# One rotation of eight tags for the operand tiles of the down projection

## The chip, the cores and the metric

The kernel runs on one core of a Trainium2 chip. Five engines work side by side, each through its own list of instructions in order: TensorE (PE) multiplies, ScalarE (ACT), VectorE (DVE) and GpSimd (POOL) work element by element, and SyncE's queue (SP) starts the transfers. Weight loads into TensorE are shown as PEld. The metric is the device time of one execution in microseconds. Three executions of the kernel before took 1674.23, 1678.88 and 1683.34 us; the median is 1678.88 us. One more execution was recorded by the profiler, and all rows below are from it.

## The reference

One encoder block over 1024 tokens of width 1024 in float32: two attentions, gated and merged, then a squared-ReLU MLP, then a gated embedding term and a last norm. The part that matters here is the MLP's second product:

```python
h2 = rmsnorm(x, g_mlp[i])
u = jax.nn.relu(jnp.einsum("bsd,df->bsf", h2, w_up[i]))      # w_up   1024 x 4096
x = x + jnp.einsum("bsf,fd->bsd", u * u, w_down[i])           # w_down 4096 x 1024
```

## The kernel before

Every float32 matrix product is done as three passes of a shorter format. An operand is split into a high part (a cast on ACT, line 1113) and a low part (the operand minus its high part, line 1114), and `mm3` (line 123) multiplies high by high, high by low and low by high into one PSUM sum.

The up projection writes the squared activations, and sums and differences of their blocks ("operand sums"), to a scratch tensor `u_d` in DRAM. The sums are made in five rotating SBUF tiles named `us`, in the pool `fp`; line 1062 sends them out.

The down projection walks over four chunks `c` of 1024 hidden columns. In each chunk Winograd's form of Strassen's scheme makes 7 block products in place of 8, in the order 1, 2, 5, 6, 3, 7, 4. A block product sums over four steps `k`; a step needs one left operand (`da`, from the tiles `ua` loaded from `u_d`) and one right operand (`db`, from `w_down` in the tiles `wd`, or from a sum or difference of its blocks that POOL makes in place, line 1200). Each operand, high and low part together, is one tile of the pool `dp`. A step is 12 matmuls of 512 columns, a block product is 48, all four chunks are 28 block products and 224 operand tiles. When a product is done, its PSUM sums are added to an accumulator `acc` on DVE (line 1144), or in chunk 0 for products 1, 5, 6 and 7 copied to it on ACT (line 1142). In the last chunk the accumulators are also added to one another on DVE and POOL (line 1093), and then the norm of the next stage begins (line 1101).

Operand tile number `n` (counted in program order, from 0) takes the tag `d0` to `d9` that line 1112 names. Every tag has one buffer, so a new tile of a tag waits until TensorE has finished with the old one. The pool `dp` is opened when `fp` is closed, and its tiles lie where `fp`'s tiles lay; the tiles that come to lie on `us` tiles can be written only when the transfers out of these have ended. A scheduler puts every engine's instructions into an order ahead of time, with its own estimate of when a tile is free; on the chip each engine then keeps to that order.

Where the text below says "pair k of product i", it means the two operand tiles of step k, `da` and `db`, with their two casts on ACT and two subtractions on DVE. In the first product of chunk 0 the first two pairs' subtractions are on POOL.

Of the kernel before, what the change touches and what calls it, by code (L numbers as in the profile page):

```python
# [10 lines left out]
F32R = mybir.dt.float32r  # L11
# [8 lines left out]
P = 128  # L20
# [33 lines left out]
def hybrid_block_kernel(ctx: ExitStack, tc, x, p, g_mix, w_in, g_qa, w_qb, g_kva, w_kvb, g_qn, g_kn,  # L54
# [34 lines left out]
    def raw_tile(name, shape):  # L89
        return wpool.tile(shape, F32, tag="raw", name=f"raw_{name}")  # L90
# [422 lines left out]
    with tc.tile_pool(name="ap", bufs=2, reuse_waits="tile") as ap:  # L513
# [273 lines left out]
        for i in range(NK + 2):  # L787
# [3 lines left out]
            d = i - 2  # L791
# [35 lines left out]
    with tc.tile_pool(name="op", bufs=2, reuse_waits="tile") as op:  # L827
# [115 lines left out]
        for n, f in enumerate((0, 2, 1)):  # L943
            t = raw_tile(f"early{f}", [P, NK, P])
# [162 lines left out]
    with tc.tile_pool(name="dp", bufs=1, reuse_waits="tile") as dp:  # L1107
        def operand(name, raw, eng):
            n = nd[0]
            nd[0] += 1  # L1110

            t = dp.tile([P, 2, 512], F32R, tag=f"d{n % 8 if n < 24 else (n - 16) % 10}", name=f"d{name}")
            act.copy(t[:, 0], raw)  # L1113
            eng.tensor_tensor(t[:, 1], raw, t[:, 0].bitcast(F32), ALU.subtract)  # L1114
            return t

        def product(i, c, av, bv):
# [34 lines left out]
            for k in range(4):  # L1152
                eng = pool if c == 0 and i == 1 and k < 2 else dve
                ab.append((operand(f"a{k}_{i}_{c}", av[k // 2][:, k % 2], eng), operand(f"b{k}_{i}_{c}", bv[:, k], eng)))
                if whole:
                    continue
                for s in range(4):
                    if k == 0:
                        room(s)
                    part(s, k, k + 1)  # L1160
                    if k == 3:
                        put(s)
# [205 lines left out]
```

## Time and profile before

| | |
|---|---|
| median of three runs | 1678.88 us (1674.23 to 1683.34) |
| the profiled execution | 1672.75 us, its span 1671.0 us |
| PE busy | 1559.7 us, 93% of the span |
| DVE busy | 1215.2 us, 73% |
| ACT busy | 815.5 us, 49% |
| POOL busy | 730.1 us, 44% |
| mean granted TensorE clock | 0.974 of 2.4 GHz |

The span runs from the first to the last instruction, and the other 1.75 us of the execution lie around it. Times in the rows count from the start of the span. The down projection runs from about 1197 us to about 1534 us. A granted clock of 1.00 is 2.4 GHz, one of 0.50 is 1.2 GHz, and a value between them is a mean over a stretch that has both.

### The profile page before, as it was taken

Reading aid. Unit: us, or ns where it says so; the run is one execution under the profiler, and the core shown is the slowest. Engines: PE = TensorE matmul, PEld = TensorE weight load, DVE = VectorE, ACT = ScalarE, POOL = GpSimd, SP = SyncE. Lnnn points to the kernel's source line nnn. Section 1 sums busy time; section 2 is a strip of 40 time slices with the busy share of each in tenths; the row PEclk is TensorE's granted clock in tenths of the full one; section 3 lists DMA queues with packets and bytes.
Section 4 is the critical chain, followed back from the end, with each engine's and each line's share of the span. In section 5 each row is a group of like instructions: output and inputs, shape, how many; then the busy total and the mean of one; then the engine's idle time right before and its main releaser. Section 6 shows DMA issues by size and latency. Waiting matters only on the chain.

```text
span 1671.0 us, 24113 instructions
## 1 busy us (share of the span) xinstructions
PE 1559.7 (93%) x8490; PEld 1320.2 (79%) x8490; DVE 1215.2 (73%) x1967; ACT 815.5 (49%) x1583; POOL 730.1 (44%) x463
## 2 busy tenths in 40 slices
PE   7999989998989888899996999999969999998898
PEld 6998877776767566688995888888758888877898
DVE  7278227776888888655467999999666878898753
ACT  6344337776988787533354222222245444435443
POOL 4254004645777777422154433333521322254653
PEclk9999999999999998999997999999979999999999
DMA  6023558999999999945544444444946353311242
GB/s 228 26 51 109 142 160 169 213 186 201 207 180 195 201 191 199 244 150 189 174 131 125 158 157 150 158 141 140 374 148 228 101 189 110 139 64 64 89 130 73
DMA packets 437865, 262.56 MB, mean 157 GB/s; under 512 B 284520, under 2 KB 383472, under 8 KB 437360
## 3 DMA queue, kind: packets, MB, share of 16 engines
q1 hardware_dynamic: 436464, 258.92, 59.2%
q10 hardware_dynamic: 1280, 2.10, 0.6%
q8 instruction: 67, 1.10, 0.3%
q14 instruction: 54, 0.44, 0.1%
HBM read 142.41 MB, written 49.35 MB: 115 GB/s over the span
## 4 chain that ended last, share of the span: by engine, by line
PE 48%; DMA 12%; DVE 10%; ACT 5%; issue 4%; POOL 4%; SPq 1%; POOLq 0%; ACTq 0%; DVEq 0%
PE u L126 17%; PE d L126 15%; DMA PT<-hl 7%; PE y L126 4%; PE wo L126 4%; PE pg L126 3%; POOL hl L602 2%; PE av L772 2%; PE gt L126 1%; ACT p L594 1%; ACT hl L600 1%; DMA wd<-in_w_down_dram 1%; DVE db L1114 1%; DVE p L591 1%; DMA bc<-rs_d 1%
## 5 line engine op out<-in xcount | busy, mean ns | idle before, releaser
L602 POOL TENSOR_TENSOR hl<-p,hl 128x1024 f16<-128x1024 f32 x128 | 279.8, 2193 | 194.8 <-PE gt L126 80.5
L126 PE MATMUL d<-db,da 128*128 128x512 f32 x1344 | 312.6, 395 | 23.3 <-ACT db L1113 16.6
L126 PEld LDWEIGHTS d<-db,da 128*128 128x128 f32 x1344 | 255.8, 191 | 79.4 <-ACT db L1113 17.0
L126 PE MATMUL u<-H_t,wop 128*128 128x512 f32 x768 | 183.6, 395 | 5.8 <-ACT H_t L900 4.6
L126 PEld LDWEIGHTS u<-H_t,wop 128*128 128x128 f32 x768 | 146.1, 191 | 38.2 <-ACT H_t L900 5.0
L591 DVE TENSOR_SCALAR_CACHE_REDUCE p<-s 128x1024 f32<-128x1024 f32 x128 | 155.6, 1218 | 16.1 <-PE s L126 5.6
L1113 ACT CAST da<-ua 128x512 fp32r<-128x512 f32 x112 | 69.6, 623 | 174.6 <-PE d L126 142.9
L594 ACT ACTIVATE p<-p,mx 128x1024 f32<-128x1024 f32 x128 | 147.2, 1150 | 9.5 <-DVE Va L458 1.5
L126 PE MATMUL u<-H_b,wop 128*128 128x512 f32 x576 | 138.2, 393 | 7.2 <-ACT wop L815 7.2
L126 PEld LDWEIGHTS u<-H_b,wop 128*128 128x128 f32 x576 | 109.4, 190 | 30.4 <-ACT wop L815 7.6
L1114 DVE TENSOR_TENSOR da<-ua,da 128x512 fp32r<-128x512 f32 x110 | 90.0, 819 | 58.2 <-ACT da L1113 58.2
L1200 POOL TENSOR_TENSOR wd<-wd,wd 128x1024 f32<-128x1024 f32 x16 | 39.8, 2492 | 195.3 <-DVE db L1114 187.4
L601 DVE TENSOR_SCALAR_CACHE_REDUCE hl<-p 128x512 f16<-128x512 f32 x128 | 87.2, 681 | 49.2 <-DMA PT<-hl 34.5
L1114 DVE TENSOR_TENSOR db<-wd,db 128x512 fp32r<-128x512 f32 x110 | 113.5, 1032 | 0.0
L126 PE MATMUL s<-KT,QT 96*128 96x512 f32 x384 | 103.5, 410 | 7.1 <-DVE p L591 6.8
L1057 POOL TENSOR_TENSOR us<-uq 128x512 f32<-128x512 f32 x15 | 19.6, 1308 | 192.9 <-DVE uq L1053 192.9
L126 PE MATMUL gt<-hH,lo_g 128*128 128x512 f32 x256 | 102.4, 400 | 1.5 <-DVE lo_g L105 1.5
L126 PE MATMUL gt<-hH,hi_g 128*128 128x512 f32 x256 | 101.9, 398 | 0.8 <-ACT hi_g L103 0.8
L126 PE MATMUL gt<-hL,hi_g 128*128 128x512 f32 x256 | 101.2, 395 | 0.0
L105 DVE TENSOR_TENSOR lo_g<-raw_g,hi_g 128x1024 fp32r<-128x1024 f32 x32 | 46.1, 1441 | 66.9 <-ACT hi_g L103 66.8
L600 ACT CAST hl<-p 128x512 f16<-128x512 f32 x128 | 78.7, 616 | 27.4 <-DMA PT<-hl 25.5
L126 PEld LDWEIGHTS s<-KT,QT 96*128 96x128 f32 x384 | 69.6, 193 | 25.2 <-DVE p L591 10.0
(341 smaller groups left out, 3930.7 us busy)
## 6 DMA issues: line engine op xcount, KB each, us to landing
ua<-u_d SPq DMA_DIRECT2D x56, 512.0 KB, 3.8
raw_g<-in_w_in_dram SPq DMA_DIRECT2D x32, 512.0 KB, 4.2
raw_up<-in_w_up_dram SPq DMA_DIRECT2D x32, 512.0 KB, 4.8
u_d<-us SPq DMA_DIRECT2D x64, 256.0 KB, 2.1
wd<-in_w_down_dram SPq DMA_DIRECT2D x16, 1024.0 KB, 9.7
u_d<-uq SPq DMA_DIRECT2D x48, 256.0 KB, 2.0
gates_d<-gst SPq DMA_DIRECT2D x32, 256.0 KB, 2.7
gg<-gates_d SPq DMA_DIRECT2D x16, 512.0 KB, 3.1
```

The source lines that it names most:

```text
L105: eng.tensor_tensor(lo, raw, hi.bitcast(F32), ALU.subtract)
L126: return [pe.matmul(ps, a, b, start=start and i == 0, stop=stop and i == len(m) - 1) for i, (a, b) in list(enumerate(m))[first:last]]
L591: dve.tensor_scalar(e, ps, 1.0, 3e38, op0=ALU.mult, op1=ALU.min, accum_out=mx)
L594: act.activation(e, e, AF.Exp, bias=mx, scale=-1.0, accum_out=sums[:, hd, qt:qt + 1])
L600: act.copy(hl[:, 0, :CUT], e[:, :CUT])
L601: dve.tensor_scalar(hl[:, 0, CUT:], e[:, CUT:], 1.0, 0.0, op0=ALU.mult, op1=ALU.max, accum_out=top)
L602: pool.tensor_tensor(hl[:, 1], e, hl[:, 0], ALU.subtract)
L772: pe.matmul(av[:, :256], values(hd, kt), PT[(2 * g + half) % 3][:, n, kt], start=(kt + n == 0), stop=(kt + n == NS))
L1057: eng.tensor_tensor(v[1], q[:, 2], q[:, 3], ALU.add)
L1113: act.copy(t[:, 0], raw)
L1114: eng.tensor_tensor(t[:, 1], raw, t[:, 0].bitcast(F32), ALU.subtract)
L1200: pool.tensor_tensor(o[:, ks], a[:, ks], b[:, ks], ALU.subtract)
```

## The change

All operand tiles now take the eight tags `d0` to `d7` in turn. Before, that held for the first 24 tiles (products 1, 2 and 5 of chunk 0); the tiles after them took ten tags in turn, beginning with `d8` and `d9`. The tiles `d8` and `d9` no longer exist.

```diff
         def operand(name, raw, eng):
             n = nd[0]
             nd[0] += 1
-
-            t = dp.tile([P, 2, 512], F32R, tag=f"d{n % 8 if n < 24 else (n - 16) % 10}", name=f"d{name}")
+            t = dp.tile([P, 2, 512], F32R, tag=f"d{n % 8}", name=f"d{name}")
             act.copy(t[:, 0], raw)
             eng.tensor_tensor(t[:, 1], raw, t[:, 0].bitcast(F32), ALU.subtract)
             return t
```

The scheduler orders the instructions anew. In the names below the digit behind `da` or `db` is the step k, the next one the product, the next one the chunk: `da0_6_0` is the left operand of step 0 of product 6 in chunk 0. Lines have moved up by one.

ACT, the casts from the end of product 1 of chunk 0 on, before:

```order
L1113 CAST db2_1_0_11597<-wd0_0_11295 128x512
L1113 CAST da3_1_0_11612<-ua0_11294 128x512 [waits DVE_49]
L1113 CAST db3_1_0_11615<-wd0_0_11295 128x512 [waits Pool_49]
L1113 CAST da0_6_0_11796<-ua2_0_0_11549 128x512 [waits DMAHW3_49,DMAHW4_49,DMAHW2_49,DMAHW5_49,DMAHW0_49,DMAHW6_49,DVE_49,Pool_49]
L1113 CAST da0_2_0_11634<-ua0_11294 128x512 [waits PE_49,Pool_49]
```

And the same place with the change:

```order
L1112 CAST db2_1_0_11597<-wd0_0_11295 128x512
L1112 CAST da3_1_0_11612<-ua0_11294 128x512 [waits DVE_49]
L1112 CAST db3_1_0_11615<-wd0_0_11295 128x512 [waits Pool_49]
L1112 CAST da0_2_0_11634<-ua0_11294 128x512 [waits DMAHW6_49,PE_49,Pool_49]
L1112 CAST db0_2_0_11637<-wd0_0_11295 128x512 [waits DMAHW1_49,Pool_49]
```

The cast for tile 24 (product 6, the first tile with tag `d8`) stood ahead of all casts of product 2 and waited for six transfer semaphores; with the change it stands behind all casts of product 5.

DVE in the last chunk, from the adds of product 2 to the first pair of product 3, before (`acc0<-acc0,d2` is the add of product 2's sum):

```order
L1144 TENSOR_TENSOR acc0_11537<-acc0_11537,d2_3_2_13419 128x1024
L1114 TENSOR_TENSOR da0_6_3_13576<-ua2_3_0_13320,da0_6_3_13576 128x512
...
L1114 TENSOR_TENSOR da2_6_3_13614<-ua2_3_1_13322,da2_6_3_13614 128x512
L1114 TENSOR_TENSOR db2_6_3_13617<-wd3_0_12738,db2_6_3_13617 128x512
L1144 TENSOR_TENSOR acc3_11541<-acc3_11541,d5_3_0_13496 128x512
L1114 TENSOR_TENSOR da3_6_3_13632<-ua2_3_1_13322,da3_6_3_13632 128x512
L1114 TENSOR_TENSOR db3_6_3_13635<-wd3_0_12738,db3_6_3_13635 128x512
L1144 TENSOR_TENSOR acc3_11541<-acc3_11541,d5_3_1_13500 128x512
...
L1114 TENSOR_TENSOR db0_3_3_13669<-wd3_1_13313,db0_3_3_13669 128x512
```

And with the change:

```order
L1143 TENSOR_TENSOR acc0_11537<-acc0_11537,d2_3_2_13419 128x1024
L1113 TENSOR_TENSOR da3_5_3_13548<-ua3_3_1_13318,da3_5_3_13548 128x512
L1113 TENSOR_TENSOR db3_5_3_13551<-wd3_0_12738,db3_5_3_13551 128x512
...
L1143 TENSOR_TENSOR acc3_11541<-acc3_11541,d5_3_0_13496 128x512
L1113 TENSOR_TENSOR da2_6_3_13614<-ua2_3_1_13322,da2_6_3_13614 128x512
...
L1113 TENSOR_TENSOR db2_6_3_13617<-wd3_0_12738,db2_6_3_13617 128x512
...
L1113 TENSOR_TENSOR da3_6_3_13632<-ua2_3_1_13322,da3_6_3_13632 128x512
L1113 TENSOR_TENSOR db3_6_3_13635<-wd3_0_12738,db3_6_3_13635 128x512
L1093 TENSOR_TENSOR acc0_11537<-acc0_11537,acc3_11541 128x512 x2
L1113 TENSOR_TENSOR da0_3_3_13666<-ua4_3_0_13570,da0_3_3_13666 128x512
```

Pair 3 of product 5 now stands behind product 2's adds, and pairs 2 and 3 of product 6 behind the adds of product 5 with which they were interleaved or which followed them. In the same way the last pair of most products now stands behind the adds of the product before it; in the last chunk so does that of product 4, behind two adds of 1024 columns for product 7.

POOL in the last chunk, before:

```order
L1200 TENSOR_TENSOR wd3_0_12738<-wd3_1_13313,wd3_0_12738 128x1024
L1093 TENSOR_TENSOR acc0_11537<-acc0_11537,acc2_11536 128x512 x4
L1200 TENSOR_TENSOR wd3_0_12738<-wd3_0_12738 128x1024
L1093 TENSOR_TENSOR acc1_11539<-acc1_11539,acc3_11541 128x512 x4
```

And with the change:

```order
L1093 TENSOR_TENSOR acc0_11537<-acc0_11537,acc2_11536 128x512 x4
L1199 TENSOR_TENSOR wd3_0_12738<-wd3_1_13313,wd3_0_12738 128x1024
L1093 TENSOR_TENSOR acc1_11539<-acc1_11539,acc3_11541 128x512
L1199 TENSOR_TENSOR wd3_0_12738<-wd3_0_12738 128x1024
L1093 TENSOR_TENSOR acc1_11539<-acc1_11539,acc3_11541 128x512 x3
```

The second half of the right operand of product 6 (`wd3_0<-wd3_1,wd3_0`) now stands behind four adds of accumulators and no longer ahead of them.

## Rows read from the trace of the kernel before

**Rows 1.** Page, part 5: the matmuls of the down projection, their idle time.

```profile
L126 PE MATMUL d<-db,da 128*128 128x512 f32 x1344 | 312.6, 395 | 23.3 <-ACT db L1113 16.6
```

**Rows 2.** PE by stretch: length, busy (matmuls), granted clock, DMA share, GB/s.

```profile
1197.00:1208.00 11.00, 11.00 (x49) 1.00 1.04 433
1208.00:1225.00 17.00, 0.42 (x2) 0.62 0.90 342
1225.00:1236.00 11.00, 10.90 (x40) 0.81 0.05 10
1236.00:1247.00 11.00, 11.00 (x50) 1.00 0.31 96
1302.00:1379.00 77.00, 77.00 (x341) 1.00 0.45 152
1490.00:1500.00 10.00, 8.77 (x32) 0.83 0.00 0
```

**Rows 3.** Timeline around the gap: start, duration, engine, operation [idle before, releaser].

```profile
1197.03 11.04 PE L126 MATMUL d<-db,da 128*128 128x512 f32 x48
1202.55 0.69 DVE L1114 TENSOR_TENSOR db<-wd,db 128x512 fp32r<-128x512 f32 x1
1203.37 4.76 POOL L1200 TENSOR_TENSOR wd<-wd,wd 128x1024 f32<-128x1024 f32 x2 [7.86 <-PE d L126]
1208.09 4.64 POOL L1200 TENSOR_TENSOR wd<-wd 128x1024 f32<-128x1024 f32 x2
...
1218.57 0.32 SPq L1062 DMA_DIRECT2D u_d<-us  x1
1222.94 1.14 ACT L1113 CAST da<-ua 128x512 fp32r<-128x512 f32 x2 [23.73 <-DMA u_d<-us]
1224.65 37.56 PE L126 MATMUL d<-db,da 128*128 128x512 f32 x154 [16.58 <-ACT db L1113]
```

**Rows 4.** SyncE's queue: loads issued for products 2, 5, 6 and 3.

```profile
1173.45 1.72 SPq L991 DMA_DIRECT2D ua<-u_d  x2
...
1192.10 0.44 SPq L991 DMA_DIRECT2D ua<-u_d  x1
1194.13 0.37 SPq L991 DMA_DIRECT2D ua<-u_d  x1
1210.99 0.53 SPq L991 DMA_DIRECT2D ua<-u_d  x1
```

**Rows 5.** DMA issued 1210.9 to 1211: KB each, us to landing.

```profile
ua<-u_d SPq DMA_DIRECT2D x1, 512.0 KB, 10.7
```

**Rows 6.** DVE and POOL around the start of chunk 1.

```profile
1289.04 2.73 POOL L1200 TENSOR_TENSOR wd<-wd 128x1024 f32<-128x1024 f32 x1
...
1289.43 2.88 DVE L1114 TENSOR_TENSOR db<-wd,db 128x512 fp32r<-128x512 f32 x1
1292.24 0.68 DVE L1114 TENSOR_TENSOR da<-ua,da 128x512 fp32r<-128x512 f32 x1
...
1293.44 2.34 DVE L1144 TENSOR_TENSOR acc<-acc,d 128x1024 f32<-128x1024 f32 x2
```

**Rows 7.** Waits, 1190 to 1550 us: total, times, longest.

```profile
ACT da L1113 <- PE d L126: 142.9, 91, 6.0
```

**Rows 8.** All engines by stretch, last chunk: PE, PEld, DVE, ACT, POOL, clock, DMA.

```profile
1456.00:1530.00 74.00, 67.39 (x281) 54.22 (x280) 69.83 (x79) 28.49 (x50) 35.74 (x20) 0.93 0.20 64
```

**Rows 9.** Timeline of the last chunk: POOL's adds, a DVE operand beside them, PE's three waits.

```profile
1471.70 6.85 POOL L1093 TENSOR_TENSOR acc<-acc,acc 128x512 f32<-128x512 f32 x4
...
1475.63 1.78 DVE L1114 TENSOR_TENSOR db<-wd,db 128x512 fp32r<-128x512 f32 x1
...
1491.23 24.32 PE L126 MATMUL d<-db,da 128*128 128x512 f32 x99 [2.59 <-DVE db L1114]
...
1517.95 1.81 PE L126 MATMUL d<-db,da 128*128 128x512 f32 x6 [2.40 <-DVE db L1114]
...
1521.39 4.64 PE L126 MATMUL d<-db,da 128*128 128x512 f32 x10 [1.62 <-DVE db L1114]
```

## Prediction

> **What bounds the kernel now.** I read the page's costliest groups first, then the stretches of the down projection with busy time and clock, then the timeline around the one gap, and last the order of the engines that feed TensorE.
>
> The group of the 1344 matmuls of the down projection is the costliest on PE, and of its 23.3 us of idle time 16.6 us are one wait, for an ACT cast [rows 1]. By stretches PE is busy all the time before and after that wait: 341 matmuls in 77 us, so 77.00/341 = 0.226 us each, 10.8 us for a product of 48 and 2.71 us for a step of 12 [rows 2]. So chunks 0 to 2 are bound by PE except for one gap, which lies behind the first product. The last chunk is different: there DVE is busy 69.83 of 74 us [rows 8] and PE waits three times for a DVE operand, 2.59, 2.40 and 1.62 us [rows 9].
>
> What makes the gap? Product 1 runs from 1197.03 for 11.04 us; the next matmul starts at 1224.65, after 16.58 us of idle time. ACT sits idle for 23.73 us until 1222.94, and the releaser is a transfer out of the `us` tiles [rows 3]. The order of ACT shows which instruction sits there: the cast for tile 24, pair 0 of product 6, with the first use of tag `d8`. It waits for six transfer semaphores, because `d8` lies on `us` tiles, and the last transfer out of these was issued only at 1218.57 [rows 3]. All casts of product 2 stand behind it. Their own inputs were there: when ACT came free at 1222.94, cast after cast ran, and PE started 1.71 us later.
>
> **The change, part by part.** The sum is made for the profiled execution, 1672.75 us (span 1671.0 and 1.75 us around it), and then moved to the median of the three runs, 1678.88 us, which lies 6.13 us above it.
>
> *The wait goes: -18.6 us.* With the change, pair 0 of product 2 follows the casts of product 1 directly. It takes `d0`, which PE has left after the first step of product 1, about 1197.03 + 2.7 = 1199.8. The cost of the gap is its idle time, 16.58 us, and what the clock did to the matmuls after it. In the 11 us from 1225 on, with a granted clock of 0.81, PE made 40 matmuls, and at 0.226 us each 11 us hold 48.7; the 8.7 missing ones are 8.7 x 0.226 = 2.0 us [rows 2]. The mean of 0.81 lies between the level of 1.2 GHz and that of 2.4 GHz, and what went before is the 17 us in which PE was busy for 0.42. Without the gap both terms go. Ends: 16.6 us (the clock falls anyway) and 18.6. I take 18.6.
>
> *What is late next.* Product 2 needs loads that were issued from 1173.45 on [rows 4], 26 us ahead, and a free ACT; DVE is through with product 1 at 1202.55 + 0.69 = 1203.2 [rows 3]. Product 5 would start at about 1218.7, product 6 at 1229.6, product 3 at 1240.4. Their loads from `u_d` were issued at 1192.10, 1194.13 and 1210.99 [rows 4]; the last of them landed after 10.7 us, at 1221.7 [rows 5], 19 us ahead of its use. The block differences for product 5 end on POOL at 1203.37 + 4.76 = 1208.1. SyncE's order is unchanged, so these transfers don't move. I cost this at nothing; the slack of about 10 us for product 5 and 19 us for product 3 hides it.
>
> *A new neighbour in chunk 0: +1.0 us.* POOL's four block differences from 1203.37 to 1212.73 [rows 3] ran while DVE had nothing to do. Now they run beside the subtractions of product 2. Beside such an operation a subtraction took 2.88 us, and 0.68 us alone [rows 6], so about one gets through per POOL operation: three of the four for pairs 0 and 1 wait, and pair 1, wanted at 1207.9 + 2.7 = 1210.6, ends near 1211.6. Ends: 0, and 4 x 2.2 = 8.8 us if none of the delay were covered; I take 1.0.
>
> *One pair less of run-ahead in chunks 0 to 2: +1.5 us.* With ten tags five pairs can be ready or in use, with eight four. A pair's two casts and two subtractions need 2.5 us undisturbed (1.14 us for two casts [rows 3], two subtractions of 0.68 [rows 6]). With eight tags a pair is freed three steps, 3 x 2.71 = 8.1 us, before its successor is wanted. In between DVE may have two adds of 2.34 us together and one or two blocked subtractions of 2.88 [rows 6]: 2.5 + 2.34 + 2 x 2.2 = 9.2 us at worst, 1.1 us too late; with one blocked, 7.0 us, in time. The nearest row is the stretch from 1236 to 1247: products 2 and 5 already use the eight tags, the blocked subtractions are there, and PE is busy for 11.00 of 11 us [rows 2]. ACT waits for PE 91 times, 142.9 us in all [rows 7]: it has time and lacks only room. Ends for the 18 products: 0, and 18 x 2.2 = 40 us if every one paid a whole blocked subtraction. I take 1.5 us, near the row.
>
> *The last chunk: +4.7 us.* DVE has no time left there, and its order now puts the last pair of a product behind the adds of the product before. After product 5 ends, DVE has four adds of about 0.6 us (half of 1.17), two accumulator adds and four subtractions until pair 3 of product 6 is ready. Beside POOL's adds each of these six takes up to 1.78 us [rows 9]: 2.4 + 6 x 1.78 = 13.1 us. PE wants the pair 8.1 us after that end. That is 5.0 us late, and in its place goes the wait of 2.59 us at product 3: +2.4. Product 4's last pair stands behind two more adds, 2.34 us [rows 6]: +2.3. POOL also makes the second half of product 6's right operand only after four adds, 6.85 us [rows 9]; that delay runs beside the same 13.1 us of DVE and I add nothing for it. Ends: -6.6 (the three waits go, because another order happens to fit) and +10 (the whole 6.85 us shows, and the clock drops once more: the stretch from 1490 holds 32 matmuls where 8.77 busy us hold 38.8, so 6.8 x 0.226 = 1.5 us [rows 2], and again the 1.62 us of the smallest wait).
>
> Sum: -18.6 + 1.0 + 1.5 + 4.7 = -11.4 us. The profiled execution becomes 1661.4, the median 1667.5 us.
>
> **The rivals.** *The tail takes it back (within 0.5%).* The gap goes, but the last chunk and the short run-ahead pay 10 us or more: -18.6 + 1.0 + 4 + 9 = -4.6, so 1674 us. For it: DVE at 69.83 of 74 us, with POOL and DVE delaying each other. Against: pairs that are late there make later waits shorter, since DVE's total work is the same.
>
> *Another wait stands behind the first (no change).* If not the tag but the transfers hold the restart, product 2 or 5 would wait until the queue is empty, near 1222.9, and the time stays at about 1679 us. For it: the DMA share is 0.90 in the gap [rows 2]. Against: the loads for product 5 had been issued by 1192.10 [rows 4], 30 us before that. This is also the case in which the change doesn't do what it says.
>
> *Bubbles at every product (slower).* With four pairs, each product of chunks 0 to 3 could wait for its last pair, which now stands behind the adds. PE has 25 products after the first three; at 18.6/25 = 0.74 us each the gain is gone, and at the 1.1 us of the worst case above the sum is -18.6 + 25 x 1.1 = +8.9, so 1688 us. For it: 9.2 against 8.1 us. Against: not every pair meets two blocked subtractions, since POOL has eight block differences for the 28 pairs of a chunk, and the stretch from 1236 to 1247 shows eight tags without a wait. The Trainium skill, Perfetto Trace Analysis, Optimization Strategy, says that the same gap repeating on the engine that should be saturated can mean that there isn't enough on-chip memory, by buffer count, for the next tile. It speaks against taking buffers away; in this trace such gaps are absent in chunks 0 to 2, with ten tags and, between products 2 and 5, with eight.
>
> **How the numbers follow.** The forecast, with the gap gone and 10 us or less paid back, has 0.69. The tail that pays nearly all back has 0.19, the second wait behind the first 0.06, bubbles at every product 0.06. About 0.5%, 8.4 us, is what a measurement of this kernel can tell from no change; faster by more than that means below 1670.5. A small part of the forecast (0.02) ends above that bound and as much of the tail's below it, so faster is 0.69, within 0.5% 0.25, slower 0.06. The range reaches down to 1659 us, where almost nothing of the 18.6 is paid back, and up to 1677 us, which takes in the tail's 1674 and leaves out the other two.
>
> **What would show it.** Right: ACT's idle time of 23.73 us before a cast is gone, PE runs from product 1 into product 2 with a pause of at most 2 us and a granted clock of 1.00 from 1208 to 1236, and the last chunk has longer waits of PE for DVE than 6.6 us in all, above all inside product 6. Wrong: a gap of several us at product 2, 5 or 6 with a transfer as its releaser; waits for `db` or `da` at product after product in chunks 1 and 2; or a last chunk whose waits are shorter than before. The sum fails if these waits together come near 18 us.

## The result, and the profile after

The median went from 1682.20 us (five runs, 1674.23 to 1683.83) to 1661.19 us (five runs, 1659.42 to 1669.97). The ratio is 0.9895, with a 95% interval of 0.9859 to 0.9931: faster by about 1%. The forecast was 1667.5 us within 1659 to 1677.

The profiled execution of the changed kernel is its longest, 1669.97 us (span 1668.2, granted clock 0.980), only 2.78 us below that of before. That doesn't contradict the median. The first matmul of product 1 started at 1207.43 us in it and at 1197.03 before [rows 3], and in the runs below at anything from 1198.65 to 1207.48, with the same matmuls in the same order ahead of it. What follows the down projection differs less: from the end of the stretch defined below to the end of the span it is 128.8 to 130.5 us in all ten profiles. So the whole time carries a scatter of several us from stages that the change doesn't touch. What the change does is read between two fixed points behind that: from the first matmul of product 1 in chunk 0 to the first one of the gate product (`pg`), which follows the down projection. Call it the stretch. Before it lasted 1541.49 - 1197.03 = 344.46 us. Its two ends after, and every piece between them (PE, timeline: start, duration, operation, count, [idle before, releaser]):

```profile
1207.43 13.99 PE L126 MATMUL d<-db,da 128*128 128x512 f32 x61
1222.71 3.01 PE L126 MATMUL d<-db,da 128*128 128x512 f32 x12 [1.29 <-DVE db L1113]
1226.11 250.53 PE L126 MATMUL d<-db,da 128*128 128x512 f32 x1103 [0.39 <-DVE db L1113]
1479.12 0.73 PE L126 MATMUL d<-db,da 128*128 128x512 f32 x2 [2.48 <-ACT db L1112]
1480.25 3.24 PE L126 MATMUL d<-db,da 128*128 128x512 f32 x13 [0.40 <-DVE db L1113]
1486.42 2.79 PE L126 MATMUL d<-db,da 128*128 128x512 f32 x11 [2.93 <-DVE db L1113]
1489.92 23.44 PE L126 MATMUL d<-db,da 128*128 128x512 f32 x102 [0.71 <-DVE db L1113]
1513.72 1.66 PE L126 MATMUL d<-db,da 128*128 128x512 f32 x6 [0.36 <-DVE db L1113]
1517.05 1.09 PE L202 MATMUL nt_ple<-ident,acc 128*128 128x128 f32 x8 [1.67 <-DVE acc L1101]
...
1522.91 8.02 PE L126 MATMUL d<-db,da 128*128 128x512 f32 x28 [3.00 <-DVE db L1113]
...
1538.80 0.36 PE L126 MATMUL pg<-hi_pg,h3H 128*128 128x256 f32 x1
```

The stretch is 1538.80 - 1207.43 = 331.37 us, 13.1 us shorter; the sum of the forecast was -11.4. Three things are to be seen. The gap of 16.58 us behind product 1 is gone, and product 2 waits 1.29 and 0.39 us for its own pairs. Then 1103 matmuls follow without a listed wait: with 61 and 12 ahead of them they end at the 1176th, which is the middle of product 6 in the last chunk (its 48 begin at the 1153rd). And there four waits come together, 2.48 + 0.40 + 2.93 inside product 6 and 0.71 at the first pair of product 3, 6.52 us in all, where before one of 2.59 stood [rows 9].

The page's group that answers to [rows 1] has lost the ACT cast as the main cause:

```profile
L126 PE MATMUL d<-db,da 128*128 128x512 f32 x1344 | 309.1, 391 | 11.7 <-DVE db L1113 9.1
```

Stretches of PE around products 1, 2 and 5 of chunk 0, one in chunk 1, and two of the last chunk (columns as in [rows 2]):

```profile
1207.00:1218.00 11.00, 11.00 (x50) 1.00 1.05 434
1218.00:1226.00 8.00, 6.43 (x28) 1.00 1.00 384
1226.00:1237.00 11.00, 10.89 (x48) 1.00 0.83 314
1312.00:1389.00 77.00, 77.00 (x342) 1.00 0.44 150
1476.00:1490.00 14.00, 7.49 (x30) 1.00 0.10 37
1490.00:1514.00 24.00, 23.64 (x103) 1.00 0.14 45
```

Where the clock had been 0.62 and 0.81 it is 1.00, with PE at work and a DMA share of 0.83 to 1.05. Around product 2 the new neighbours are seen. POOL makes its first two block differences, each in two operations. The first subtraction of pair 0 begins before them and takes 0.68 us; the second one, both of pair 1 and the first one of pair 2 run beside them and take four times as long (POOL and DVE, timeline):

```profile
1213.56 0.68 DVE L1113 TENSOR_TENSOR da<-ua,da 128x512 fp32r<-128x512 f32 x1
...
1213.78 5.54 POOL L1199 TENSOR_TENSOR wd<-wd,wd 128x1024 f32<-128x1024 f32 x2 [7.86 <-PE d L126]
1214.17 2.89 DVE L1113 TENSOR_TENSOR db<-wd,db 128x512 fp32r<-128x512 f32 x1
...
1216.98 2.89 DVE L1113 TENSOR_TENSOR da<-ua,da 128x512 fp32r<-128x512 f32 x1
...
1219.28 5.62 POOL L1199 TENSOR_TENSOR wd<-wd 128x1024 f32<-128x1024 f32 x2
...
1219.79 2.87 DVE L1113 TENSOR_TENSOR db<-wd,db 128x512 fp32r<-128x512 f32 x1
...
1222.58 2.87 DVE L1113 TENSOR_TENSOR da<-ua,da 128x512 fp32r<-128x512 f32 x1
```

In the last chunk, inside product 6 (POOL, ACT and DVE, timeline):

```profile
1470.18 5.93 POOL L1093 TENSOR_TENSOR acc<-acc,acc 128x512 f32<-128x512 f32 x4
...
1476.08 2.34 POOL L1199 TENSOR_TENSOR wd<-wd,wd 128x1024 f32<-128x1024 f32 x1
...
1479.10 1.10 DVE L1113 TENSOR_TENSOR db<-wd,db 128x512 fp32r<-128x512 f32 x1 [6.04 <-ACT db L1112]
...
1480.72 2.29 DVE L1093 TENSOR_TENSOR acc<-acc,acc 128x512 f32<-128x512 f32 x1
...
1482.93 1.77 DVE L1113 TENSOR_TENSOR da<-ua,da 128x512 fp32r<-128x512 f32 x1
1484.62 1.74 DVE L1113 TENSOR_TENSOR db<-wd,db 128x512 fp32r<-128x512 f32 x1
```

Pair 3 of product 6 is ready at 1484.62 + 1.74 = 1486.36, and PE goes on at 1486.42: its wait of 2.93 us is for DVE. The wait of 2.48 us before it hangs on pair 2, whose right operand POOL began to make only at 1476.08, behind the four adds. But the two waits aren't independent: the subtraction for that operand stands ahead of pair 3 in DVE's order, and DVE was idle for 6.04 us until the cast of it was there. So here POOL's lateness holds up DVE, and through DVE pair 3. The waits, over the whole down projection (total, times, longest), show POOL's and DVE's part, and that ACT still waits for room above all, as in [rows 7]:

```profile
ACT da L1112 <- PE d L126: 147.2, 93, 5.0
...
ACT db L1112 <- POOL wd L1199: 11.4, 4, 9.3
...
PE d L126 <- DVE db L1113: 9.1, 7, 3.0
```

### The profile page after: what moved, and what is told of

It is laid out like the page before. It is cut to its first block, busy times and chain, and to the rows that moved or that the text cites. A ratio compares the mean times of both kernels' runs of the same rounds, so it can differ in the third digit from the quotient of the medians.

```text
span 1668.2 us, 24110 instructions
## 1 busy us (share of the span) xinstructions
PE 1557.8 (93%) x8490; PEld 1317.4 (79%) x8490; DVE 1222.8 (73%) x1967; ACT 816.4 (49%) x1583; POOL 735.1 (44%) x463
## 4 chain that ended last, share of the span: by engine, by line
PE 45%; DVE 7%; issue 2%; POOL 2%; DMA 1%; ACT 1%; SPq 0%; POOLq 0%; DVEq 0%; ACTq 0%
PE u L126 18%; PE d L126 14%; PE wo L126 6%; PE pg L126 3%; PE y L126 3%; POOL wd L1199 1%; DVE da L1113 1%; DVE db L1113 1%; PE pp L126 1%; DVE acc L1093 1%; DVE acc L1297 0%; DVE acc L1143 0%; DMA gg<-gates_d 0%; DVE sg L1295 0%; POOL acc L1093 0%
## 5 line engine op out<-in xcount | busy, mean ns | idle before, releaser
L126 PE MATMUL d<-db,da 128*128 128x512 f32 x1344 | 309.1, 391 | 11.7 <-DVE db L1113 9.1
L1113 DVE TENSOR_TENSOR da<-ua,da 128x512 fp32r<-128x512 f32 x110 | 102.0, 927 | 29.3 <-ACT da L1112 29.2
L1199 POOL TENSOR_TENSOR wd<-wd,wd 128x1024 f32<-128x1024 f32 x16 | 43.5, 2719 | 177.4 <-DVE db L1113 169.6
L1113 DVE TENSOR_TENSOR db<-wd,db 128x512 fp32r<-128x512 f32 x110 | 106.1, 965 | 6.0 <-ACT db L1112 6.0
L772 PE MATMUL av<-PT,Va 128*128 128x256 f16 x512 | 68.2, 287 | 22.0 <-DMA PT<-hl 20.9
```

What stands on the lines that cost most here:

```text
L126: return [pe.matmul(ps, a, b, start=start and i == 0, stop=stop and i == len(m) - 1) for i, (a, b) in list(enumerate(m))[first:last]]
L772: pe.matmul(av[:, :256], values(hd, kt), PT[(2 * g + half) % 3][:, n, kt], start=(kt + n == 0), stop=(kt + n == NS))
L1199: pool.tensor_tensor(o[:, ks], a[:, ks], b[:, ks], ALU.subtract)
```

## The experiments

Each run is read by the stretch, since its scatter seems small: a second profile of the changed kernel gave 331.51 against 331.37; no other kernel has two profiles. Theory A below is the forecast's: ACT takes its casts in order, and a cast that waits for memory under the `us` tiles stood ahead of product 2's. Theory D says that in the last chunk POOL's order makes the waits, E that DVE's chain of adds does. The diffs show the lines that matter; of a line that names a tag only the tag is shown, and "..." stands for what is left out.

| kernel | stretch, us | median, us | ratio to before, 95% |
|---|---|---|---|
| before | 344.46 | | |
| changed kernel | 331.37 | 1661.19 | 0.9895 (0.9859 to 0.9931) |
| the same again (e5) | 331.51 | 1664.38 | 0.9928 (0.9906 to 0.9951) |
| ten tags, casts in another order (e1) | 327.45 | 1662.37 | 0.9908 (0.9873 to 0.9943) |
| ten tags from tile 56 (e2) | 346.89 | 1681.93 | 1.0020 (1.0002 to 1.0039) |
| ten tags from the start (e4) | 353.47 | 1685.87, one run | |
| ten tags in the last chunk alone (e6) | 328.48 | 1663.13 | 0.9913 (0.9896 to 0.9930) |
| six tags (e7) | 338.83 | 1670.50, one run | |
| eight tags, POOL's adds later (e3) | 333.50 | 1665.17 | 0.9922 (0.9891 to 0.9953) |
| as e3, without four adds of DVE (e8) | 328.08 | 1657.31, one run | |

**e1: order alone.** The kernel before keeps its ten tags; only the casts of tiles 24 and 25, the first on `d8` and `d9`, are ordered behind the cast of tile 23. In the engines' orders only these two casts on ACT and their two subtractions on DVE have moved.

```diff
-            act.copy(t[:, 0], raw)
+            ins = act.copy(t[:, 0], raw)
+            if n == 23:
+                hold[0] = ins
+            if n in (24, 25):
+                follow(ins, hold[0])
```

> Tags as in the kernel before (ten from tile 24 on), but the two casts of pair 0 of product 6 in chunk 0 are put behind the last cast of product 5 in ACT's order. Theory A (the gap was ACT held in order behind tile 24, which lies on the operand sums): the gap of 16.6 us after product 1 is gone with ten tags too; from the first matmul of product 1 to the first of the gate product 344.5 us become about 327.5 (344.5 - 18.6 + 1.7), 4 us less than with eight tags (331.4), since the last chunk keeps the order of the kernel before. Theory B (it is the place of the two extra tags that costs, wherever the casts stand): the gap stays, about 344 us.

The stretch is 327.45 us, 17.0 below the kernel before. The same cast with the same six semaphores to wait for now stands behind product 5's casts (ACT, timeline):

```profile
1232.85 0.62 ACT L1113 CAST da<-ua 128x512 fp32r<-128x512 f32 x1 [0.26 <-DMA u_d<-us]
```

It runs 1232.85 - 1207.48 = 25.4 us after the start of product 1, against 1222.94 - 1197.03 = 25.9 before [rows 3]: the transfers let go of the memory at nearly the same time. What changed is who stands behind the cast. It waited 23.73 us with product 2 behind it, and now 0.26 with nothing late. So A holds: the gap came neither from the number of tags nor from the transfers alone, but from the place of that cast in ACT's order. What is left of PE's waits (timeline):

```profile
1222.50 3.02 PE L126 MATMUL d<-db,da 128*128 128x512 f32 x12 [1.03 <-DVE db L1118]
1225.90 256.23 PE L126 MATMUL d<-db,da 128*128 128x512 f32 x1128 [0.38 <-DVE db L1118]
1484.71 24.35 PE L126 MATMUL d<-db,da 128*128 128x512 f32 x99 [2.58 <-DVE db L1118]
```

Product 2's 1.03 + 0.38 come with ten tags as with eight. The last chunk has its old wait of 2.58.

**e2: the extra tags later.** Eight tags in turn up to tile 55, that is through chunk 0, and ten from the first tile of chunk 1.

```diff
-tag=f"d{n % 8}"
+tag=f"d{n % 8 if n < 56 else (n - 48) % 10}"
```

> Eight tags for chunk 0 (tiles 0 to 55), ten after that. Theory A: as the run before, no gap, about 327.5 us from product 1 to the gate product, so about 4 us less than the changed kernel, since by chunk 1 the operand sums have long been sent. Theory C (eight or ten tags make no difference behind chunk 0): 331 us as in the changed kernel.

This was a miss of the expectation, and the most telling run. The stretch was 346.89 us, with a gap as before, and longer (ACT and PE, timeline):

```profile
1231.78 0.62 ACT L1113 CAST db<-wd 128x512 fp32r<-128x512 f32 x1 [26.09 <-DMA u_d<-us]
1233.48 263.95 PE L126 MATMUL d<-db,da 128*128 128x512 f32 x1153 [18.94 <-ACT db L1113]
```

The order of ACT shows why (with the semaphores that each cast waits for):

```
L1113 CAST db3_1_0_11615<-wd0_0_11295 128x512 [waits Pool_49]
L1113 CAST db0_1_1_12154<-wd1_0_11553 128x512 [waits DMAHW5_49,DMAHW1_49,DMAHW6_49,DMAHW0_49,DMAHW7_49,DVE_49,Pool_49]
L1113 CAST da0_2_0_11634<-ua0_11294 128x512 [waits PE_49,Pool_49]
```

The cast of chunk 1's first right operand, tile 57, was put in the very place where tile 24's had stood. It is the first tile on `d9`, and 33 tiles further on in the program than tile 24; it sits ahead of product 2, presumably because the scheduler takes its unused tag to be free and its data is there (how the scheduler chooses isn't shown). The theory stands, my idea of how to avoid the gap by a later start fell: also from 33 tiles further on, a first use of an extra tag was drawn forward to this place. From tile 168 on it was not (e6).

**e4: the extra tags at once.** All tiles take ten tags in turn, so that the first tile on `d8` is product 2's own first operand.

```diff
-tag=f"d{n % 8}"
+tag=f"d{n % 10}"
```

> Ten tags from the first tile on, so tiles 8 and 9, pair 0 of product 2, lie on the operand sums. Theory A: product 2 itself must wait for the transfers out of these sums, whatever ACT's order; the gap after product 1 stays at 16 to 18 us, product 1 to the gate product about 344 us. If the gap came from the cast standing too early alone, it would be gone, about 328 us.

ACT waited 23.58 us for the same transfers and 1.36 more for the second tile, and PE 25.08 us. The stretch was 353.47 us (PE, timeline):

```profile
1228.89 272.21 PE L126 MATMUL d<-db,da 128*128 128x512 f32 x1187 [25.08 <-ACT db L1113]
```

The memory under `d8` and `d9` is really not free until some 25 us after product 1 begins: the first cast ran at 1226.24, which is 25.8 us behind 1200.47. But A's figure of 344 us was missed by 9: a gap at the end of product 1 would have been about as long as before, and this one is 8.5 us longer. PE's order shows where it stands (`d1_0_2` is a sum of product 1, `d2_0_0` one of product 2):

```
L126 MATMUL d1_0_2_11569<-db1_1_0_11579,da1_1_0_11576 128x512
L126 MATMUL d2_0_0_11640<-db0_2_0_11637,da0_2_0_11634 128x512 [waits Activation_49]
...
L126 MATMUL d1_0_0_11562<-db1_1_0_11579,da1_1_0_11576 128x512 [waits Pool_49]
```

Four matmuls of product 2's first pair were drawn forward into product 1, behind its 14th, and the 34 others of product 1 stood behind them. So A's mechanism shows once more, on PE itself: an instruction that waits for this memory is placed too early, and what stands behind it pays. On ACT the casts stand in the program's order here, so the wait of 23.58 us is for the memory itself.

**e6: the extra tags in the last chunk alone.** Ten tags from tile 168 on.

```diff
-tag=f"d{n % 8}"
+tag=f"d{n % 8 if n < 168 else (n - 160) % 10}"
```

> Eight tags for chunks 0 to 2 (tiles 0 to 167), ten in the last chunk. Theory A: by tile 168 no cast can be put early enough to wait for the operand sums, so there is no gap; the last chunk has its old order. Product 1 to the gate product about 327.5 us, 4 us less than the changed kernel, and the time as much less. Theory C (ten tags in the last chunk gain nothing by themselves): about 331 us.

The stretch is 328.48 us, 2.9 shorter than with eight tags. There is no gap in chunk 0, and in the last chunk one wait stands at product 3, as with ten tags (PE, timeline):

```profile
1480.85 22.74 PE L126 MATMUL d<-db,da 128*128 128x512 f32 x99 [2.59 <-DVE db L1114]
1507.81 2.93 PE L126 MATMUL d<-db,da 128*128 128x512 f32 x6 [4.21 <-DVE v_ple L167]
```

The 99 matmuls behind that wait took 22.74 us, where e1 has 24.35, but the wait behind them was 4.21 us, where e1 has 2.36 for the same releaser: what the faster matmuls gained there was waited away. By e1 and e6 the eight tags cost about 3 to 4 us, nearly all of it in the last chunk. By their whole times e1, e6 and the changed kernel can't be told apart (the intervals overlap); by the stretch both are ahead of it.

**e7: six tags.** If the run-ahead mattered in chunks 0 to 2, three pairs would show it more than four.

```diff
-tag=f"d{n % 8}"
+tag=f"d{n % 6}"
```

> Six tags throughout, three pairs. A pair is then freed 5.4 us ahead of its use; two casts and two subtractions (2.5 us), two adds (2.34) and one blocked subtraction (2.2) make 7.0 us, so each product that meets a block difference on POOL should wait about 1.6 us: PE waits for DVE in chunks 1 and 2 too, 10 to 40 us in all, 341 to 371 us from product 1 to the gate product. If the number of tags costs only in the last chunk, chunks 1 and 2 stay without a wait and the stretch takes 333 to 336 us.

```profile
1208.76 240.61 PE L126 MATMUL d<-db,da 128*128 128x512 f32 x1057 [2.88 <-DVE db L1114]
1450.60 14.36 PE L126 MATMUL d<-db,da 128*128 128x512 f32 x62 [1.22 <-DVE db L1114]
...
1482.09 24.35 PE L126 MATMUL d<-db,da 128*128 128x512 f32 x96 [5.96 <-DVE db L1114]
```

One wait of 2.88 us inside product 1, then 1057 matmuls without one, through chunks 1 and 2 and into the last chunk, where the waits come back larger than with eight tags. The stretch of 338.83 us lies between the two ranges expected: chunks 1 and 2 did as the second said, and what it has above that one lies in product 1 of chunk 0 and in the last chunk. "Bubbles at every product" is out for eight tags, since it doesn't come with six. The Trainium skill, Perfetto Trace Analysis, Optimization Strategy, reads a repeated gap on the engine that should be saturated as a possible lack of room for the next tile. No run here had such a repeated gap in chunks 1 and 2; the single long gap came with more room, not with less.

**e3: POOL's order in the last chunk.** POOL's adds for product 2 move behind the block differences for product 6, as they stood before. D expects most of the waits in product 6 to go.

```diff
-                    pool.tensor_tensor(o[:, ks], a[:, ks], b[:, ks], ALU.subtract)
+                    diff[0] = pool.tensor_tensor(o[:, ks], a[:, ks], b[:, ks], ALU.subtract)
...
-                    add(pool, 2, 1, s)
...
             t2 = minus(t1, b22, t1)
+            if last:
+                for s in range(4):
+                    follow(add(pool, 2, 1, s), diff[0])
```

> The changed kernel, but in the last chunk POOL makes the second half of product 6's right operand ahead of its four adds of accumulators, as in the kernel before. Theory D (of the last chunk's loss, the part inside product 6 is POOL's order: ACT's cast waits 9.3 us for that half): PE's waits inside product 6, 6.5 us in the changed kernel, fall below 3 us, and product 1 to the gate product takes about 328 us. Theory E, that of the prediction (DVE's own chain of adds and blocked subtractions behind product 5 sets it): they stay at 5 us or more, 331 us.

```profile
1475.01 2.79 PE L126 MATMUL d<-db,da 128*128 128x512 f32 x11 [2.77 <-DVE db L1113]
1481.74 25.97 PE L126 MATMUL d<-db,da 128*128 128x512 f32 x102 [3.94 <-DVE db L1113]
```

ACT's longest wait for POOL fell from 9.3 to 3.9 us. Inside product 6 PE's waits did fall below 3 us, as D asked, from 5.81 to 2.77. But a wait of 3.94 us came at the first pair of product 3, where the changed kernel has 0.71, so they sum to 6.71 against 6.52, and both have DVE as the releaser. DVE's rows show how the wait moved: it is idle 2.94 us and no longer 6.04, and then POOL's adds run beside its own work (DVE, timeline):

```profile
1465.88 1.12 DVE L1113 TENSOR_TENSOR db<-wd,db 128x512 fp32r<-128x512 f32 x1 [2.94 <-ACT db L1112]
...
1472.12 2.83 DVE L1113 TENSOR_TENSOR db<-wd,db 128x512 fp32r<-128x512 f32 x1
1474.87 3.47 DVE L1093 TENSOR_TENSOR acc<-acc,acc 128x512 f32<-128x512 f32 x2
```

The 1203rd matmul, in product 3, starts 281.86 us after product 1 in e3 and 282.49 in the changed kernel, nearly the same. The stretch, 333.50 us, is 2.1 longer than the changed kernel's because of what lies behind that point: the 102 matmuls there took 25.97 us, where the changed kernel has 23.44, at a lower granted clock (PE by stretch, columns as in [rows 2]):

```profile
1482.00:1508.00 26.00, 25.71 (x102) 0.90 0.13 41
```

So D falls in what it costs: POOL's order decides which pair is late, and not how much is lost. That POOL's lateness runs beside DVE's work, as the forecast had it, isn't what the changed kernel does, since DVE stands idle for it there.

**e8: DVE's chain.** As e3, and the four adds of `acc3` to `acc0` on DVE (the sum of product 5 into block 3) are left out.

```diff
-                    add(dve, 3, 5, s)
```

> As the run with POOL's adds later, and the four adds of accumulator 5 to accumulator 3 on DVE in the last chunk are left out (part of the output is missing). Theory E (DVE's chain behind product 5 sets the wait at products 6 and 3, 6.7 us in that run): two of these adds lie in the chain and two behind it, 2 to 4 x 1.78 us, so the wait falls to 3 us or less and product 1 to the gate product from 333.5 to about 329 us. If DVE's chain is not it, both stay.

DVE's order at this place is e3's with these adds missing. PE's waits from product 5 to product 3 (timeline):

```profile
1465.79 3.02 PE L126 MATMUL d<-db,da 128*128 128x512 f32 x12 [0.39 <-DVE db L1113]
1469.19 3.01 PE L126 MATMUL d<-db,da 128*128 128x512 f32 x12 [0.38 <-DVE db L1113]
1473.68 3.06 PE L126 MATMUL d<-db,da 128*128 128x512 f32 x12 [1.48 <-DVE db L1113]
1477.07 23.73 PE L126 MATMUL d<-db,da 128*128 128x512 f32 x103 [0.33 <-DVE db L1113]
```

They sum to 2.58 us where e3 has 6.71, and the stretch falls by 5.4 us, from 333.50 to 328.08. So with POOL's half made early, DVE's chain sets the waits, and E holds for that order. The adds' own length in e3 is 1.19 + 0.68 + 3.47 = 5.3 us, of which 4.1 showed in these waits. The fall of the stretch is not all theirs: behind the waits the clock was higher than in e3, and 103 matmuls took 23.73 us:

```profile
1477.00:1501.00 24.00, 23.73 (x103) 1.00 0.14 45
```

**e5: the changed kernel once more,** to see what two profiles of one kernel differ by, and to time it beside e6.

> The changed kernel as it is, beside the next one on the same chip. Product 1 to the gate product about 331 us; time about 0.99 of the kernel before.

The waits repeat to a few hundredths (1.25, 0.38, 2.49, 0.41, 2.93, 0.69), and the stretch to 0.14 us. The median was 1664.38 us, 13.4 below the 1677.73 of before on the same chip.

## Why the prediction was right

**The wait goes, -18.6: right.** The gap is gone, the clock behind it is 1.00 (x48 to x50 matmuls in 11 us, where [rows 2] has x40), and e1 gives the size with little else altered: 17.0 us less, plus the 1.4 of product 2's new waits, 18.4.

**What is late next, nothing: right.** Product 5 and product 6 of chunk 0 started without a wait, and the rival "another wait stands behind the first" is out. The DMA share of 0.90 that spoke for it didn't hold PE up: after, PE works in the same place at shares of 1.05, 1.00 and 0.83.

**The new neighbour in chunk 0, +1.0: right mechanism, undersized.** It cost 1.29 + 0.39 = 1.7 us of waits. Three of the four subtractions for pairs 0 and 1 were blocked, as I had it, and pair 1 was 1.29 us late in place of 1.0: POOL's two pairs of operations took 5.54 and 5.62 us where alone they had 4.76 and 4.64 [rows 3]. What I left out is that the first subtraction of pair 2 is blocked as well; that is the 0.39.

**One pair less of run-ahead, +1.5: wrong.** It cost nothing in chunks 0 to 2, and one pair fewer again costs nothing in chunks 1 and 2 (e7). My worst case put two adds and two blocked subtractions between a free pair and its use in every product. The row that I named as the nearest, 11.00 of 11 us with eight tags [rows 2], was the better guide.

**The last chunk, +4.7: near in sum, wrong in both its parts.** e1 has the gap gone and the last chunk of before, so the eight tags cost 331.37 - 327.45 = 3.9 us, of which 0.3 are the longer waits of product 2 (1.68 against 1.41). It can be divided at the 1203rd matmul, in product 3. In e1 that is the second one behind the restart at 1484.71, which 1201 precede, so at 1484.94, or 277.46 us from the start of product 1; after, 1489.92 - 1207.43 = 282.49. So 5.0 us were lost up to there, 0.3 of them in product 2 of chunk 0 and the rest at products 6 and 3, where I had +2.4, and 1.1 us came back behind it, where I had +2.3 for product 4. That the two add up to about what I forecast is luck.

The mechanism of the first part was only half right. I let DVE's own adds and subtractions make pair 3 late and added nothing for POOL, because its delay would run beside them. The rows show both a pair behind POOL and one behind DVE late in turn, with DVE idle for 6.04 us in between. The nothing for POOL's order was right as a price, since e3, where ACT's wait for POOL is 3.9 us and no longer 9.3, loses about as much up to the 1203rd matmul; the reason that I gave for it was not. That the adds on DVE are what is paid when POOL is early, e8 shows.

Of the second part, product 4's waits did grow, from 2.40 + 1.62 [rows 9] to 0.36 + 1.67 + 3.00 us, but by 1.0 and not 2.3, and PE's matmuls ran faster than before. Before, in the place of the changed kernel's 1.00 from 1490 to 1514 (PE by stretch, columns as in [rows 2]):

```profile
1490.00:1516.00 26.00, 24.32 (x99) 0.93 0.13 41
```

How much of the 1.1 us this clock gave back isn't shown: in e6 the same 99 matmuls ran at 1.00, and the next wait grew by as much as they had gained.

"The tail takes it back" asked for 9 us in the last chunk; it took less than 4.

In sum, e1's -17.0 and the 3.9 for eight tags make the measured -13.1 (they must, as differences of the same three stretches), against -11.4. The medians, 21.0 us apart in the first comparison and 13.4 in the second, both hold -13.1 in their intervals (-23.7 to -11.6 and -15.8 to -8.2); the forecast's -11.4 lies just outside the first and inside the second. The larger difference of medians is presumably helped by the scatter ahead of product 1.

## What to carry to other kernels

Before adding buffers, look at whose memory they lie on and at what place in an engine's order the first instruction that takes them ends up: one cast that waits for such memory holds up everything behind it, though its own result isn't wanted for 20 us. Ordering that cast later gains as much as giving the buffers up, and 3.9 us of the stretch more (e1), because it keeps them for the one place that uses them. In the last chunk, moving work from before a late operand to behind it moved the wait and didn't shorten it (e3), since POOL's adds then ran beside other operations of DVE. To judge a change whose gain is less than 1%, measure between two fixed instructions around it, because the stages ahead of it can move the whole time by more.

## What the runs showed that I had not expected

The same kernel's product 1 started between 1200.79 and 1207.43 us in two profiles of it, though everything from there to the gate product agreed within 0.14 us. So the scatter of whole times comes from the stages ahead. In the chains of work that ended last of these two profiles the 717 matmuls of `wo`, well ahead of the MLP, begin at 781.10 and 787.88 us, 6.8 us apart already; what makes the difference before that, I have not traced.

POOL pays too when it meets DVE: two of its operations went from 4.76 to 5.54 us beside the subtractions. The Trainium skill, SBUF — State Buffer, Who interferes with whom, has a VectorE instruction with two SBUF inputs contend with a GpSimd instruction that reads SBUF, and lets the order of issue decide who is blocked. The rows agree that they contend: 2.89 us for a subtraction beside POOL, 0.68 alone [rows 6], and POOL's own operations longer by 0.4 to 0.5 us each. The role of the order of issue no run here shows.

The granted clock did not fall after the 6.5 us of waits in products 6 and 3. PE was busy for 7.49 of 14 us there at 1.00, and for the next 24 us the clock stayed at 1.00. Before, a stretch from 1490 to 1516 behind a single wait of 2.59 us had 0.93 on average, while e6 had 1.00 behind the same wait (1480 to 1504) and 0.62 in the stretch after it (1504 to 1516). What decides it in these short stretches the runs don't show.
